# Two transformer layers with a mixture of experts: weights re-laid in DRAM as the chunks of one load, and experts ranked by their rows and packed in double, full, half and quarter tiles

## The chip, the cores and the metric

The kernel runs on one core of a Trainium2 chip. The metric is the device time of one execution in microseconds; its traces are taken by the hardware profiler in an execution of its own. Engines are called as the profile calls them: PE multiplies matrices, PEld loads their stationary operand, DVE, ACT and POOL work on vectors, SP issues most DMAs.

## The reference, cut to what matters

Two layers over 256 latent tokens and 256 context tokens of width 1024. Layer 0 mixes with a gated delta rule beside an S5 scan, layer 1 with latent attention; each layer ends in the same kind of expert stage. Layer 0 sends all 512 tokens through it, layer 1 the 256 latent ones only.

```python
def grouped_moe(h, router_w, router_bias, w_gate, w_up, w_down):
    tok = h.reshape(-1, h.shape[-1])
    scores = jax.nn.sigmoid((tok @ router_w).astype(F32))
    ...                                   # best group of 4 experts, then TOP_K = 2 experts in it
    gates = jnp.sum(jax.nn.one_hot(idx, N_EXPERTS, dtype=F32) * wts[..., None], axis=1)
    out = jnp.zeros(tok.shape, F32)
    for e in range(N_EXPERTS):            # 16 experts, w_gate and w_up 1024 x 512, w_down 512 x 1024
        act = jax.nn.silu(tok @ w_gate[e]) * (tok @ w_up[e])
        out = out + gates[:, e:e + 1] * (act @ w_down[e])
    return out.reshape(h.shape).astype(h.dtype)
```

Everything is fp32. One expert's weights are 6.29 MB, all of a layer's 100.7 MB. With the inputs used, the experts of layer 0 get 36, 55, 46, 43, 99, 80, 71, 52, 72, 47, 27, 58, 132, 51, 78 and 77 rows in the order of their numbers, and those of layer 1 get 23, 44, 31, 6, 47, 60, 50, 17, 34, 11, 42, 45, 17, 19, 27 and 39 (counted from the reference).

## The kernel before, in words

The program is one stream: adaLN vectors, the mixer of layer 0, `moe_route` and `experts0`, the mixer of layer 1, `moe_route` and `experts1`, a final norm. A scheduler puts the instructions of each engine in an order before the launch; within an engine they run in that order. Weights come through rings of buffers of 8 KB per partition (`chunk()`, tag `ch`, 1 MB each): `load_chunk` (L199) takes the next buffer of the ring and issues the load on SP, which stands there until the buffer is free. In layer 0's expert stage nine buffers serve the weights, in layer 1's eighteen.

All loads of big weights fetch from the matrix in its own layout: partition p of a chunk of w_gate takes rows p, 128+p, 256+p and 384+p, 512 columns each, so 2 KB at a time from rows that lie next to each other (`gate_up_chunk`); for w_down the 2 KB are halves of 4 KB rows (`down_chunk`). The input projection (`w_in_load`) takes 512 B at a time, its u part 1 KB. The adaLN weights ada_w alone come as whole rows, 8 KB for each partition.

`moe_route` computes, with many small operations on DVE and a few matmuls, every token's two experts, the row counts `num`, and each row's place in the tiles (`dif`, `val`, `rank`). Then come `tok`, `gate` and row lists for each tile (`m.toki`, `m.gate`, `m.rowi`).

**Layer 0** (`experts0`) has 17 tiles of 128 rows: one per expert, and two for one expert with over 128 rows, which changes places with expert 8 (`BIGP`). A tile's rows are gathered from DRAM (`gather`, on POOL's queue), transposed on PE (`turn`, L203) and split in a rounded part and a remainder (`split`, tags `sp`). Each weight chunk is split too (`wsplit`: `hi` on ACT at L1660, `lo` on DVE or POOL at L1661), in three pairs of buffers (`HI`), and three matmuls replace one (`mm3`). A chunk of 128x2048 is four slices, so it takes 12 matmuls of 512 columns, an expert 72. The rows go back to DRAM with a scatter (`write`); the last tile's are added by matmul (`put_back`). The line `first = wsplit(...)` puts the split of the first chunk ahead of the first tile's own work.

**Layer 1** (`experts1`) has 8 tiles, each of two experts with up to 64 rows. It does not split: PE multiplies fp32 directly from the loaded chunk, one expert on 64 columns of the array, the other on the other 64 (`half`, `p[c, :]` with `j.mw` = 64). The rows are picked with one-hot matmuls (`pick`, `sl,h2k` in the trace), and added back the same way (`put_back`, `y,sT`).

Rows above an expert's capacity (128 or 64) go to overflow tiles in a loop with a count read at run time (`overflow_loop`, up to `NOV` = 7 rounds). With the counts above it runs zero rounds. In layer 0 the ids of 14 places are read from `m.exi` into a register of SP (`expert_id`, a TENSOR_LOAD); all others, and all ids of layer 1, are constants in the program.

Of the kernel before, what the change touches and what calls it, by code (L numbers as in the profile page):

```python
# [31 lines left out]
NOV = 7  # L32
# [4 lines left out]
BIGP = 8  # L37
# [58 lines left out]
def lay(a):  # L96
# [10 lines left out]
    o["w_in"] = f["ab_w_in"][0]  # L107
# [30 lines left out]
    o["q_up"] = f["mla_w_q_up"][0]  # L138
    o["kv_up"] = f["mla_w_kv_up"][0]
    o["mla_wo"] = f["mla_w_out"][0]  # L140
# [3 lines left out]
    o["wg"] = f["moe_w_gate"].reshape(32, 1024, 512)  # L144
    o["wu"] = f["moe_w_up"].reshape(32, 1024, 512)
    o["wd"] = f["moe_w_down"].reshape(32, 512, 1024)
# [14 lines left out]
def _build(es, tc, I, O):  # L161
# [29 lines left out]
    def load_chunk(src, shape, eng=nc.sync):  # L191
        n = 1
        for s in shape[1:]:
            n *= s
        t = chunk()
        v = t[:, :n]
        if len(shape) == 3:
            v = v.rearrange("p (a b) -> p a b", a=shape[1])
        eng.dma_start(v, src)  # L199
        return v  # L200
# [405 lines left out]
    def w_in_load(c0, n, rows=slice(0, D), tile=lambda: cw.tile([128, 1024], F32, tag="raw", bufs=1, name=nm("raw"))):  # L606
        w = tile()
        nc.sync.dma_start(w.rearrange("p (k n) -> p k n", n=n),
                          I["w_in"][rows, c0:c0 + n].rearrange("(k p) n -> p k n", p=128))
        return w  # L610

    def w_in_cols(c0, n, eng):
        return [w.rearrange("p (k n) -> p k n", n=n) for w in split_w(w_in_load(c0, n), eng)]
# [10 lines left out]
    with tc.tile_pool(name="xi1", bufs=1) as xi1, tc.tile_pool(name="ar", bufs=ARB) as arp:  # L624
# [4 lines left out]
        def norm0():  # L629
            for t in range(NT):  # L630
# [12 lines left out]
        uw = [w_in_load(2064 + hh * 256, 256, slice(512 * kh, 512 * kh + 512), tile)  # L643
              for hh, kh, tile in ((0, 0, chunk), (0, 1, chunk), (1, 0, chunk), (1, 1, chunk))]
# [318 lines left out]
    def glu():  # L963
        gluw = [load_chunk(I["glu_w"][:, n * 256:(n + 1) * 256].rearrange("(k p) n -> p k n", p=128), [128, 4, 256])
                for n in range(2)]
# [261 lines left out]
    def out_proj0(opening, after):  # L1227
        with tc.tile_pool(name="op0", bufs=1) as op, tc.tile_pool(name="oq0", bufs=3) as oq:
# [6 lines left out]
            def parts(n, h):  # L1235
                raw = load_chunk(I["w_out"][h * 512:(h + 1) * 512, n * 512:(n + 1) * 512].rearrange(
                    "(k p) n -> p k n", p=128), [128, 4, 512])
# [28 lines left out]
    def out_proj1(opening, after):  # L1266
        with tc.tile_pool(name="op1", bufs=1) as op, tc.tile_pool(name="oq1", bufs=3) as oq:
            def parts(n, h):
                raw = load_chunk(I["mla_wo"][h * 512:(h + 1) * 512, n * 512:(n + 1) * 512].rearrange(
                    "(k p) n -> p k n", p=128), [128, 4, 512])  # L1270
# [27 lines left out]
    def moe_open(l, stack):  # L1298
# [41 lines left out]
        if l == 0:  # L1340
            m.xes = [m.mo.tile([128, D], F32, name=f"xe{i}") for i in range(3)]
            for t in m.xes:
                G.memset(t, 0.0)
            m.io16 = m.mo.tile([128, 16], F32, name="io16")
            m.far = m.mo.tile([128, 16], F32, name="far")
            G.tensor_copy(m.io16, sm[:, SM_IO16:SM_IO16 + 16])
            G.tensor_scalar(m.far[:, 0:BIGP], m.io16[:, 0:BIGP], 16.0 - BIGP, None, op0=OP.add)
            G.tensor_scalar(m.far[:, BIGP:16], m.io16[:, BIGP:16], float(BIGP), None, op0=OP.subtract)
            G.memset(m.far[:, 0:2], -1.0)
        else:  # L1350
            m.h2 = [m.mo.tile([128, D], F32, name=nm("h2k")) for _ in range(2)]
        return m
# [31 lines left out]
    def moe_route(m):  # L1384
        l, n, mo = m.l, m.n, m.mo
        cap = CAP0 if l == 0 else CAP1
        nst = 17 if l == 0 else 8
# [67 lines left out]
        t16, ovn, ovs, dif = rt([128, 16]), rt([128, 16]), rt([128, 16]), rt([128, 16])  # L1455
        if l == 0:


            key, kmx, big, ep = rt([128, 16]), rt([128, 1]), rt([128, 16]), rt([128, 16])
            V.scalar_tensor_tensor(key, num, float(cap), m.far, op0=OP.is_gt, op1=OP.mult)  # L1460
            red(kmx, key, OP.max)
            V.tensor_scalar(big, m.far, kmx, None, op0=OP.is_equal)
            V.tensor_scalar(key[:, 0:1], kmx, 16.0 - BIGP, -16.0, op0=OP.is_ge, op1=OP.mult)
            V.scalar_tensor_tensor(m.io16[:, BIGP:BIGP + 1], kmx, float(BIGP), key[:, 0:1], op0=OP.add, op1=OP.add)
            V.scalar_tensor_tensor(key, m.io16, float(BIGP), big, op0=OP.subtract, op1=OP.mult)
            tt(ep, m.io16, key, OP.subtract)
            m.exi = rt([128, 16], I32, True)
            V.tensor_copy(m.exi, ep)
            first, caps = rt([128, 16]), rt([128, 16])
            V.scalar_tensor_tensor(first, ep, float(BIGP), ep, op0=OP.is_gt, op1=OP.add)  # L1470
            V.tensor_scalar(caps, big, 128.0, 128.0, op0=OP.mult, op1=OP.add)
            V.scalar_tensor_tensor(num, big, -128.0, num, op0=OP.mult, op1=OP.add)
        V.tensor_scalar(ovn, num, float(cap), None, op0=OP.is_gt)
        for j in range(1, 3 if l == 0 else 2):
            V.scalar_tensor_tensor(ovn, num, float(cap + 128 * j), ovn, op0=OP.is_gt, op1=OP.add)
# [23 lines left out]
        V.scalar_tensor_tensor(rin, tid, -128.0, rin, op0=OP.mult, op1=OP.add)  # L1499

# [75 lines left out]
    def gate_up_chunk(l, name, e, hh):  # L1576
        return load_chunk(wsrc(l, name, e)[hh * 512:(hh + 1) * 512, :].rearrange(
            "(k p) n -> p k n", p=128), [128, 4, 512])

    def down_chunk(l, e, nh):  # L1580
        return load_chunk(wsrc(l, "wd", e)[:, nh * 512:(nh + 1) * 512].rearrange(
            "(k p) n -> p k n", p=128), [128, 4, 512])

    def overflow_loop(m, w2, body):

        nreg = nc.values_load(m.novi[0:1, 0:1], min_val=0, max_val=NOV,
                              skip_runtime_bounds_check_because="at most 7 tiles can overflow")
        with tc.For_i(0, nreg, 1) as it:  # L1588
# [3 lines left out]
            body(it + m.nst, e)  # L1592

# [6 lines left out]
    def open_rg2():  # L1600
# [11 lines left out]
    def experts0(m):  # L1612
        with ExitStack() as st:
# [19 lines left out]
            def split(name, p, n):  # L1633
# [10 lines left out]
                return hi, lo  # L1644

# [54 lines left out]
            def half(u, name, hh, parts=None):  # L1700
# [490 lines left out]
```

## Time and profile before

| | before |
|---|---|
| time, median of 3 runs | 1413.93 us (1410.01 to 2414.91) |
| the profiled execution's own time | 1414.94 us |
| its span | 1412.7 us, granted clock 0.942 |
| PE busy | 1251.5 us, 89% |
| DVE, ACT, POOL busy | 56%, 37%, 27% |
| DMA | 340.40 MB, mean 241 GB/s |
| packets | 201805, of them 70638 under 2 KB and 201201 under 8 KB |
| layer 0's expert stage, first row transposes to last tile | 605 to 932 us |
| layer 1's, first expert matmul to last | 1161 to about 1400 us |

The page cuts the span into 40 slices of 35.3 us and gives each engine's busy share in tenths; PEclk is the clock granted to PE, in tenths of full speed. The view by windows gives the same for chosen stretches, in us from the span's start, with the number of instructions in brackets. In the timeline a row is a run of like instructions: start, length, engine, line, operation, output and inputs, tile shape (rows by columns of the array and elements), count, and in square brackets the idle time before it with what ended it. An fp32 matmul on the loaded chunk counts as two there.

### The profile page before, as it was taken

How to read it: one execution, taken by the hardware profiler on the slowest of the kernel's cores; microseconds unless marked ns; L12 is line 12 of the kernel's file. 1: busy time of each engine (PE TensorE's matmuls, PEld its weight loads, DVE VectorE, ACT ScalarE, POOL GpSimd, SP SyncE). 2: the span in 40 equal slices, each digit the busy share in tenths (PEclk: the TensorE clock that was granted, in tenths of full speed). 3: DMA queues.
4: the chain of work that ended last, by engine and by line, in shares of the span. 5: the costliest groups of instructions: out<-in, count | busy, mean ns of one | idle time of the engine just before them, and what ended most of it. 6: DMA issues, size and time to landing. Idle time of an engine off the chain costs nothing. (4 is left out here: it accounts for less than half of the span.)

```text
span 1412.7 us, 18172 instructions
## 1 busy us (share of the span) xinstructions
PE 1251.5 (89%) x6716; PEld 847.8 (60%) x6716; DVE 787.6 (56%) x1460; ACT 529.6 (37%) x775; POOL 381.0 (27%) x266
## 2 busy tenths in 40 slices
PE   5889989899788999589999999976999669999996
PEld 1786655555327988457777777744777544444422
DVE  5776756844974465767775577775566151221112
ACT  3312634544112242167776477724365011000100
POOL 1443434320126330334443233353231020000000
PEclk9999999899798999789999999998999779999998
DMA  8713457767488345679999699753034569999980
GB/s 306 257 34 88 155 171 221 225 216 235 149 251 281 131 172 180 273 244 345 377 369 330 227 317 358 283 210 113 32 135 155 194 254 385 398 401 400 399 336 31
DMA packets 201805, 340.40 MB, mean 241 GB/s; under 512 B 31726, under 2 KB 70638, under 8 KB 201201
## 3 DMA queue, kind: packets, MB, share of 16 engines
q1 hardware_dynamic: 171952, 310.97, 62.3%
q10 hardware_dynamic: 23920, 16.95, 3.9%
q0 software_dynamic: 5840, 11.28, 2.2%
q8 instruction: 55, 0.90, 0.3%
q14 instruction: 38, 0.30, 0.1%
HBM read 320.56 MB, written 27.82 MB: 247 GB/s over the span
## 5 line engine op out<-in xcount | busy, mean ns | idle before, releaser
L206 PE MATMUL ps<-hi,sp 128*128 128x512 f32 x816 | 269.5, 404 | 6.0 <-ACT sp L1640 3.7
L1661 DVE TENSOR_TENSOR lo<-ch,hi 128x2048 fp32r<-128x2048 f32 x80 | 185.1, 2330 | 84.6 <-ACT hi L1660 79.8
L1660 ACT ACTIVATE hi<-ch 128x2048 fp32r<-128x2048 f32 x96 | 184.1, 1920 | 80.3 <-PE ps L206 52.8
L206 PEld LDWEIGHTS ps<-hi,sp 128*128 128x128 f32 x816 | 154.0, 190 | 42.7 <-ACT sp L1640 4.4
L206 PE MATMUL ps<-lo,sp 128*128 128x512 f32 x408 | 164.9, 404 | 3.2 <-DVE lo L1661 2.4
L206 PE MATMUL ps<-ch,stat 128*32 128x512 f32 x384 | 93.9, 646 | 31.7 <-DMA ch<-in_ada_w 30.6
L206 PE MATMUL ps<-ch,xT 128*64 128x512 f32 x480 | 119.7, 596 | 0.0
L1661 POOL TENSOR_TENSOR lo<-ch,hi 128x2048 fp32r<-128x2048 f32 x16 | 73.9, 4621 | 160.6 <-ACT hi L1660 160.6
L206 PEld LDWEIGHTS ps<-lo,sp 128*128 128x128 f32 x408 | 77.8, 191 | 26.9 <-DVE lo L1661 8.8
L206 PEld LDWEIGHTS ps<-ch,xT 128*64 128x64 f32 x480 | 36.1, 137 | 66.5 <-issue 65.2
L228 POOL TENSOR_TENSOR frs<-rs,sm 128x1 f32<-128x1 f32 x2 | 1.1, 560 | 259.8 <-DVE rs L227 259.8
L1867 ACT ACTIVATE aT<-ps 128x512 f32<-128x512 f32 x8 | 4.8, 597 | 149.1 <-PE ps L203 149.1
L206 PE MATMUL ps<-ch,aT 128*64 128x512 f32 x240 | 60.0, 596 | 0.7 <-ACTq L1588 0.7
L1880 DVE TENSOR_TENSOR y<-ps,bcm 128x512 f32<-128x512 f32 x16 | 11.1, 691 | 81.8 <-PE ps L206 81.8
L603 POOL TENSOR_TENSOR wl<-raw,wh 128x1024 fp32r<-128x1024 f32 x16 | 38.7, 2417 | 66.2 <-ACT wh L602 66.0
L206 PE MATMUL ps<-hH,wh 128*128 128x512 f32 x128 | 55.0, 430 | 0.0
L206 PEld LDWEIGHTS ps<-ch,stat 128*32 128x32 f32 x384 | 13.6, 112 | 67.7 <-DMA ch<-in_ada_w 35.0
L206 PE MATMUL ps<-hL,wh 128*128 128x512 f32 x128 | 53.8, 420 | 0.0
L206 PE MATMUL ps<-hH,wl 128*128 128x512 f32 x128 | 53.1, 415 | 0.0
L742 DVE SCALAR_TENSOR_TENSOR ac<-ps,convw,ac 128x510 f32<-128x510 f32 (+1 forms) x48 | 35.5, 740 | 23.7 <-ACT ac L738 23.3
L1152 POOL TENSOR_TENSOR ch<-ch,ch 128x512 fp32r<-128x512 f32 (+1 forms) x28 | 31.1, 1127 | 58.3 <-ACT ch L1151 32.3
L206 PE MATMUL ps<-y,sT 128*128 128x512 f32 x80 | 40.9, 642 | 6.4 <-DVE y L1880 2.3
(543 smaller groups left out, 2559.7 us busy)
## 6 DMA issues: line engine op xcount, KB each, us to landing
ch<-in_wg SPq DMA_DIRECT2D x63, 1024.0 KB
ch<-in_wd SPq DMA_DIRECT2D x62, 1024.0 KB
ch<-in_wu SPq DMA_DIRECT2D x61, 1024.0 KB
ch<-in_ada_w SPq DMA_DIRECT2D x88, 512.0 KB
raw<-in_w_in SPq DMA_DIRECT2D x16, 512.0 KB
bcm<-modd ACTq DMA_DIRECT2D x12, 512.0 KB
x<-in_xs SPq DMA_DIRECT2D x8, 512.0 KB
yd<-x SPq DMA_DIRECT2D x8, 512.0 KB
```

The lines of the kernel that those rows point to most:

```text
L206: return T.matmul(out, l, r, start=start, stop=stop)
L228: G.tensor_tensor(out, t, bc(neghalf, [128, n]), op=OP.pow)
L603: eng.tensor_tensor(wl, w, wh.bitcast(F32), op=OP.subtract)
L742: V.scalar_tensor_tensor(ac[:, :, lo:hi], pv[:, :, lo + o:hi + o], convw[:, blk, j:j + 1], ac[:, :, lo:hi], op0=OP.mult, op1=OP.add)
L1152: eng.tensor_tensor(lo, src, hi.bitcast(F32), op=OP.subtract)
L1660: last_split[:] = (S.activation(hi, w, AF.Copy), eng.tensor_tensor(lo, w, hi.bitcast(F32), op=OP.subtract))
L1661: eng.tensor_tensor(lo, w, hi.bitcast(F32), op=OP.subtract))
L1867: S.activation(j.aT.rearrange("p k n -> p (k n)"), p, AF.Copy)
L1880: V.tensor_tensor(j.y[:, nh], p, g2[:, nh * 512:(nh + 1) * 512], op=OP.mult)
```

## The change

It has two parts.

**Layout.** `cut()` re-lays w_in, its u part (now `w_inu`), glu_w, w_out, mla_w_in, q_up, kv_up, mla_wo and the three expert weights on the host side of the program, before the launch, as blocks of 128 partitions by the contiguous elements of one load. A chunk of expert weights is then one contiguous MB, 8 KB for each partition; the w_in blocks are 4 KB for each partition. ada_w is unchanged. The number of loads, their bytes and the buffers in SBUF stay.

```diff
+    def cut(w, k, n):
+        r, c = w.shape[-2] // (128 * k), w.shape[-1] // n
+        b = w.reshape(-1, r, k, 128, c, n).transpose(0, 1, 4, 3, 2, 5)
+        return np.ascontiguousarray(b).reshape(-1, r, c, 128, k * n)
+    o["w_in"] = cut(w_in[:, 0:2048], 8, 128)[0, 0]
...
-    o["wg"] = f["moe_w_gate"].reshape(32, 1024, 512)
+    for n, w in (("wg", "gate"), ("wu", "up"), ("wd", "down")):
+        o[n] = cut(f["moe_w_" + w].reshape((32,) + f["moe_w_" + w].shape[2:]), 4, 512).reshape(32, 256, 2048)
...
     def gate_up_chunk(l, name, e, hh):
-        return load_chunk(wsrc(l, name, e)[hh * 512:(hh + 1) * 512, :].rearrange(
-            "(k p) n -> p k n", p=128), [128, 4, 512])
+        return load_chunk(wsrc(l, name, e)[hh * 128:(hh + 1) * 128, :], [128, 4, 512])
```

**Packing.** `moe_route` ranks the experts by their row counts (`key`, `cmp`, `pos`), those of `STATIC = (2, 4)` first whatever they hold: experts 0 and 1 in layer 0, 0 to 3 in layer 1. The rank is the place. `caps` and `first` give a place its capacity and first row.

Layer 0 has 13 tiles. Place 2, the fullest, has two tiles for itself (capacity 256), places 3 to 9 one each (128), and places 0 and 1, 10 and 11, 12 and 13, 14 and 15 share a tile, 64 rows each. In a shared tile nothing is split: `whole()` only copies the transposed rows, and `pair()` multiplies in fp32 directly from the loaded chunk, one expert on each 64 columns, as layer 1 does. The order is: places 0 and 1, 10 and 11, the double tile, 12 and 13, places 3, 4, 5, then 14 and 15, then 6, 7, 8, 9. The line `first` is gone.

Layer 1 has 7 tiles: places 0 to 11 in six tiles of two, and places 12 to 15 in one tile of four, 32 rows each, in the order 0, 1, 2, 3, 6, 4, 5 (6 is the tile of four). The experts' ids of all but the static places are now read at run time in layer 1 too.

With the counts above, layer 0's places hold 36 and 55; 132; 99, 80, 78, 77, 72, 71, 58; 52, 51, 47, 46, 43, 27. Layer 1's hold 23, 44, 31, 6; 60, 50, 47, 45, 42, 39, 34, 27; 19, 17, 17, 11. So the overflow loop runs zero rounds again.

```diff
+        V.scalar_tensor_tensor(key, num, 16.0, m.tie, op0=OP.mult, op1=OP.add)
+        tt(cmp, bc(key[:, None, :], SQ), bc(key[:, :, None], SQ), OP.is_gt)
+        red(pos[:, :, None], cmp, OP.add)
...
+        tt(oh, bc(sm[:, SM_IO16:SM_IO16 + 16, None], SQ), bc(pos[:, None, :], SQ), OP.is_equal)
+        tt(oh, oh, bc(sm[:, None, SM_IO16:SM_IO16 + 16], SQ), OP.mult)
+        red(key[:, :, None], oh, OP.add)
+        m.exi = rt([128, 16], I32, True)
+        V.tensor_copy(m.exi, key)
...
+            def whole(name, p, n):
+                o = w2.tile([128, n, 128], F32R, tag=f"{name}h", name=nm("wh")).bitcast(F32)
+                for i in range(n // 4):
+                    S.activation(o[:, 4 * i:4 * i + 4], p(i).rearrange("p (k n) -> p k n", k=4), AF.Copy)
+                return o
...
+            def pair(p, xT, k0, ws, n):
+                for q in range(4):
+                    for b, w in enumerate(ws):
+                        c = slice(64 * b, 64 * b + 64)
+                        mm(p[c], xT[:, k0 + q, c], w[:, q, :], k0 + q == 0, k0 + q == n - 1)
...
-            order = [[t] for t in range(BIGP)] + [[BIGP, BIGP + 1]] + [[t] for t in range(BIGP + 2, m.nst)]
+            one = {p: ([p], [p]) for p in range(3, 10)}
+            order = [([0], [0, 1]), ([10], [10, 11]), ([1, 2], [2]), ([11], [12, 13]), one[3], one[4], one[5],
+                     ([12], [14, 15]), one[6], one[7], one[8], one[9]]
...
-            first = wsplit(gate_up_chunk(0, "wg", 0, 0), V)
             fetch(1)
-            with tc.issue_after(last_split[0].ins), tc.issue_after(last_split[1].ins):
-                unit(0)
-                unit(1)
+            unit(0)
+            unit(1)
...
+            order = [0, 1, 2, 3, 6, 4, 5]
+            def fixed(i):
+                ti = order[i]
                 c = slice(ti, ti + 1)
-                return job([2 * ti, 2 * ti + 1], lambda kk, i: m.ohT[:, kk, i, c], m.tokf[:, c], m.gate[:, c])
+                return job([lambda p=p: who(p) for p in ((2 * ti, 2 * ti + 1) if ti < 6 else range(12, 16))],
+                           lambda kk, i: m.ohT[:, kk, i, c], m.tokf[:, c], m.gate[:, c])
```

Outside the two routes and the two expert stages every engine has the same instructions in the same order, with other sources in the loads. Inside them PE has 3484 rows in all instead of 3898, DVE 1318 instead of 1380, ACT 673 instead of 749, SP 624 instead of 540.

PE at the start of layer 0's experts, before: `xe` are the gathered rows, `hi` and `lo` the split weights, `sp` the split rows.

```order
L203 MATMUL ps_5017<-cm,xe_4487 128x128 x4
L203 MATMUL ps_5024<-cm,xe_4487 128x128 x4
L206 MATMUL ps_5050<-hi_5005,sp_5015 128x512
L206 MATMUL ps_5050<-lo_5006,sp_5015 128x512
L206 MATMUL ps_5087<-hi_5083,sp_5015 128x512
L206 MATMUL ps_5087<-lo_5084,sp_5015 128x512
L203 MATMUL ps_5033<-cm,xe_4488 128x128 x4
```

The same place after: `ch` are chunks as loaded, `wh` the copied rows.

```order
L208 MATMUL ps_5010<-cm,xe_4487 128x128 x4
L208 MATMUL ps_5016<-cm,xe_4487 128x128 x4
L208 MATMUL ps_5023<-cm,xe_4488 128x128 x4
L211 MATMUL ps_5038<-ch_5039,wh_5009 64x512
L211 MATMUL ps_5038<-ch_5041,wh_5009 64x512
L211 MATMUL ps_5038<-ch_5039,wh_5009 64x512
L208 MATMUL ps_5029<-cm,xe_4488 128x128 x4
```

The first matmuls of an expert no longer stand behind a split of a weight chunk on ACT and DVE; half of the second tile's transposes have moved ahead of them.

SP around the first expert loads of layer 0, from the last of four loads of the adaLN weight that stand among them, before:

```order
L199 DMA ch_4983<-in_ada_w 128x2048
L199 DMA ch_5152<-in_wg 128x4x512
L199 DMA ch_5190<-in_wd 128x4x512
L199 DMA ch_5252<-in_wu 128x4x512
L1595 TENSOR_LOAD rt_4823
L199 ISA
L199 DMA ch_5276<-in_wg 128x4x512
```

The same place after:

```order
L204 DMA ch_4983<-in_ada_w 128x2048
L204 DMA ch_5066<-in_wu 128x2048
L204 DMA ch_5076<-in_wu 128x2048
L1607 TENSOR_LOAD rt_4850
L204 ISA
L204 DMA ch_5098<-in_wg 128x2048
L1607 TENSOR_LOAD rt_4850
```

Before, ten loads of layer 0's expert weights stand ahead of the first read of an id; after, the eight of the first tile's gate and up weights. The next ones stand behind ids that the route computes.

PE in layer 1's tile of four, after: the last four of the first half of the gate matmuls, the transposes of the tile ahead of it (`act`), and the start of the second half and of the next tile's picking (`sl,h2k`). Before, each tile has two chunks in turn there, `64x512`.

```order
L211 MATMUL ps_9211<-ch_9215,xT_9120 32x512
L211 MATMUL ps_9211<-ch_9220,xT_9120 32x512
L211 MATMUL ps_9211<-ch_9225,xT_9120 32x512
L211 MATMUL ps_9211<-ch_9230,xT_9120 32x512
L208 MATMUL ps_9249<-cm,act_9208 128x128 x4
L211 MATMUL ps_9211<-ch_9255,xT_9120 32x512
L211 MATMUL ps_9286<-sl_9279,h2k_8421 128x128
```

Four experts now take turns on strips of 32 columns, so the tile has twice as many matmul instructions as a tile of two.

More of the change, by code (lines that the diff above doesn't have):

```diff
@@ L31 @@
 CAP1 = 64
-NOV = 7
+NOV = 8
 RG = 5
@@ L194, in load_chunk @@
             n *= s
[L195 to L200, printed above, removed]
+        v = chunk()[:, :n]
+        three = v.rearrange("p (a b) -> p a b", a=shape[1]) if len(shape) == 3 else v
+        eng.dma_start(v if len(src.shape) == 2 else three, src)
+        return three
     def tp(out, in_, n=128):
@@ L604, in split_w, with w_in_load @@
         return wh, wl
[L606 to L609, printed above, removed]
+    def w_in_load(src, w):
+        nc.sync.dma_start(w, src)
         return w
     def w_in_cols(c0, n, eng):
-        return [w.rearrange("p (k n) -> p k n", n=n) for w in split_w(w_in_load(c0, n), eng)]
+        raw = w_in_load(I["w_in"][c0 // n], cw.tile([128, 1024], F32, tag="raw", bufs=1, name=nm("raw")))
+        return [w.rearrange("p (k n) -> p k n", n=n) for w in split_w(raw, eng)]
     def mm3(p, ah, al, bh, bl, start, stop):
@@ L642, in _build @@
         slots[0], slots[1] = [mring], 0
-        uw = [w_in_load(2064 + hh * 256, 256, slice(512 * kh, 512 * kh + 512), tile)
-              for hh, kh, tile in ((0, 0, chunk), (0, 1, chunk), (1, 0, chunk), (1, 1, chunk))]
+        uw = [w_in_load(I["w_inu"][kh, hh], chunk()) for hh in range(2) for kh in range(2)]
         u_first = split_w(uw.pop(0), G)
@@ L1473, in moe_route @@
-        V.tensor_scalar(ovn, num, float(cap), None, op0=OP.is_gt)
-        for j in range(1, 3 if l == 0 else 2):
-            V.scalar_tensor_tensor(ovn, num, float(cap + 128 * j), ovn, op0=OP.is_gt, op1=OP.add)
+        key, pos, first, caps = (rt([128, 16]) for _ in range(4))
+        cmp, oh = (t[:, i:i + 256].rearrange("p (a b) -> p a b", a=16) for i in (0, 256))
+        SQ = [128, 16, 16]
+        V.scalar_tensor_tensor(key, num, 16.0, m.tie, op0=OP.mult, op1=OP.add)
+        tt(cmp, bc(key[:, None, :], SQ), bc(key[:, :, None], SQ), OP.is_gt)
@@ L1476, in moe_route @@
+        tt(num, num, caps, OP.subtract)
+        V.tensor_scalar(ovn, num, 0.0, None, op0=OP.is_gt)
+        for j in range(1, 4 if l == 0 else 2):
+            V.scalar_tensor_tensor(ovn, num, float(128 * j), ovn, op0=OP.is_gt, op1=OP.add)
         V.tensor_tensor_scan(ovs, ones[:, 0:16], ovn, 0.0, op0=OP.mult, op1=OP.add)
@@ L1592, in overflow_loop, with experts_of, get @@
             body(it + m.nst, e)
+    def experts_of(m):
+        ids = {p: p for p in range(STATIC[m.l])}
+        def get(p):
+            if p not in ids:
+                ids[p] = expert_id(m.exi[0:1, p:p + 1])
+            return ids[p]
+        return get
     def expert_id(ap):
@@ L1760, in experts0 @@
                 for hh in range(2):
-                    half(unit(0), name, hh, first if (name, hh) == ("wg", 0) else None)
-            for i in range(16):
+                    half(unit(0), name, hh)
+            for i in range(len(order)):
                 cur = unit(i)
@@ L1769, in experts0 @@
                             g2[c] = bc_mod(w1, 0, c, 5, f"g2{c}")
[L1770 to L1771 removed]
+                fetch(tiles.index(order[i][0][-1]) + 3)
+                nxt = unit(i + 1) if i + 1 < len(order) else None
                 if nxt:
@@ L1774, in experts0 @@
                 for j in cur:
-                    j.aT = split("a", turn(j.a), 4)
+                    j.aT = (whole if len(j.es) == 2 else split)("a", turn(j.a), 4)
                 if nxt:
                     half(nxt, "wg", 1)
-                    if i < 14 and len(nxt) == 1:
-                        job(order[i + 2][0], i + 2)
+                    if i + 2 < len(order) and len(nxt) == 1:
+                        job(order[i + 2][0][0], order[i + 2][1])
                     write(cur)
```

139 lines of the change are left out of this document (64 added, 75 removed).

## The prediction

> **What bounds the kernel now.** I began with the page's strip of 40 slices, each 35.3 us.
>
> ```profile
> PE   5889989899788999589999999976999669999996
> PEclk9999999899798999789999999998999779999998
> GB/s 306 257 34 88 155 171 221 225 216 235 149 251 281 131 172 180 273 244 345 377 369 330 227 317 358 283 210 113 32 135 155 194 254 385 398 401 400 399 336 31
> ```
>
> PE is busy nearly throughout, so what shortens PE's queue shortens the kernel, if the data keep up. In two stretches PE and the DMAs are full together: slices 18 to 26 (layer 0's experts) and 33 to 38 (layer 1's). The windows put numbers to them (us, busy time with count of PE, PEld, DVE, ACT, POOL, clock, DMA share, GB/s):
>
> ```profile
> 605.70:932.00 326.30, 313.90 (x1396) 245.84 (x1396) 226.18 (x150) 232.15 (x194) 123.80 (x46) 0.98 0.86 307
> 613.80:769.70 155.90, 154.64 (x698) 122.00 (x697) 111.27 (x74) 116.44 (x97) 57.93 (x23) 0.99 0.98 353
> 1200.00:1360.00 160.00, 158.38 (x728) 63.24 (x724) 31.89 (x57) 11.94 (x20) 0.00 (x0) 1.00 1.05 400
> 584.00:598.00 14.00, 1.22 (x10) 0.77 (x9) 13.22 (x70) 0.26 (x1) 4.88 (x3) 0.50 1.02 422
> ```
>
> In layer 0's stage PE is busy 154.6 of 155.9 us, in layer 1's 158.4 of 160.0. The DMA share is about 1 in both, but at three different rates: 353, 400 and, in the last row, 422 GB/s. That last stretch is the route of layer 0, while the first expert chunks in 2 KB pieces and adaLN weights in 8 KB pieces come in.
>
> Next the timeline, for the price of one tile in each stage.
>
> ```profile
> 880.52 0.60 PE L203 MATMUL ps<-cm,xe 128*128 128x128 f32 x4
> 889.41 0.63 PE L206 MATMUL ps<-hi,sp 128*128 128x512 f32 x2
> 890.11 0.63 PE L206 MATMUL ps<-hi,sp 128*128 128x512 f32 x2
> 899.18 0.60 PE L203 MATMUL ps<-cm,xe 128*128 128x128 f32 x4
> 1160.67 0.64 PE L206 MATMUL ps<-x,xT 128*64 128x512 f32 x1
> 1160.67 0.64 PE L206 MATMUL ps<-ch,xT 128*64 128x512 f32 x1
> 1161.15 0.59 PE L206 MATMUL ps<-x,xT 128*64 128x512 f32 x1
> 1181.91 0.66 PE L203 MATMUL ps<-cm,act 128*128 128x128 f32 x4
> 1210.94 0.65 PE L203 MATMUL ps<-cm,act 128*128 128x128 f32 x4
> 1218.88 7.09 PE L206 MATMUL ps<-ch,aT 128*64 128x512 f32 x32
> 1225.80 7.04 PE L206 MATMUL ps<-ch,xT 128*64 128x512 f32 x32
> ```
>
> A full tile of layer 0 takes 899.18 - 880.52 = **18.66 us** from one tile's transposes to the next's. Three matmuls take 890.11 - 889.41 = 0.70 us, 72 of them 16.8, and 1.86 are left for transposes. 17 x 18.66 = 317.2 us, the whole stage. In layer 1 two matmuls on 64 columns start together (1160.67 twice) and the next pair 0.48 us later, 0.43 in steady flow (7.04 / 16). A tile takes 1210.94 - 1181.91 = **29.03 us**.
>
> **The change part by part.** *Layer 0's tiles.* A shared tile costs gate and up at 7.04 each, down at 7.09 and transposes of 1.86: 23.0 us for two experts, where two full tiles cost 37.3. I take layer 1's rows because the instruction is the same: fp32, 64 columns, 512 elements. So 9 x 18.66 + 4 x 23.0 = 259.9 us against 317.2: **-57.3**.
>
> *Start of layer 0.* Before, the first matmuls stand behind splits:
>
> ```profile
> 607.90 0.50 PE L206 MATMUL ps<-hi,sp 128*128 128x512 f32 x1 [1.40 <-ACT sp L1640]
> 610.21 0.79 PE L206 MATMUL ps<-lo,sp 128*128 128x512 f32 x1 [1.81 <-DVE lo L1661]
> 790.43 0.50 PE L206 MATMUL ps<-hi,sp 128*128 128x512 f32 x1 [1.61 <-ACT sp L1640]
> 792.88 0.73 PE L206 MATMUL ps<-hi,sp 128*128 128x512 f32 x2 [1.71 <-DVE sp L1641]
> ```
>
> A shared tile needs one copy on ACT and no weight split, so steady flow begins at about 608 instead of 613: **-5** (0 to -6). At 790 the tile pair of expert 8 has stalls of 1.6 and 1.7 us with a lowered clock between; now a shared tile follows it, which waits for no remainder: **-2** (0 to -5).
>
> *Supply of layer 0.* Eight chunks are in at the start, the ring holds nine. A shared tile eats 12 chunks (12.6 MB) in 23 us, 547 GB/s, more than any window shows; a full tile six in 18.66, 337 GB/s; the double tile six in 37. Two bounds follow. First the ring: at 400 GB/s a chunk comes every 2.62 us, 8.8 in 23 us, so the first two shared tiles take the stock from 8 to 4.8 and to 1.6, and the double tile fills it again; at 353 (7.7 in 23 us) the stock runs out in the second, and each shared tile waits a few us. Second the sum: the stage moves 326.3 x 307 = 100.1 MB now, some 97 with four tiles' rows fewer, and 97 MB in 260 us are 373 GB/s; at 353 they take 275 us. So the term lies between 0 and +22 (15 by the sum, 7 for the ring). Which rate holds? Share 0.98 at 353 scales to 378 at the share of 1.05 that layer 1 reaches, and larger pieces raise that by 422/1.02 over 400/1.05, 8.6%, to 411. Both lie above 373, so I stay near the lower end, at **+5**.
>
> The Trainium skill, "DMA: Bandwidth & Descriptors", "Why small descriptors are slow (HBM only)", gives a fixed overhead of about 3 cycles a packet besides one cycle per 32 B. By it 2 KB pieces cost 67 cycles for 64 and 8 KB pieces 259 for 256, so the new layout would be worth 3.4% and not 8.6%: 391 GB/s here, still above 373, and the +5 would stand. The trace's 422 against 400 is 5.5%, between the two, though its pieces are mixed.
>
> *The route.* DVE works it off in one chain:
>
> ```profile
> 585.10 0.42 DVE L1433 TENSOR_TENSOR cmp<-rt 128x256 f32<-128x256 f32 x1
> 586.05 2.55 DVE L1435 TENSOR_TENSOR cmp<-cmp,sm 128x256 f32<-128x256 f32 x1
> 588.63 0.69 DVE L1401 TENSOR_REDUCE rt<-cmp 128x64 f32<-128x512 f32 x1
> 590.72 0.17 DVE L1460 SCALAR_TENSOR_TENSOR rt<-rt,far 128x16 f32<-128x16 f32 x1
> ```
>
> Small operations follow each other every 0.1 us or so. Layer 0 loses ten small ones and gains ten small ones, three on 256 elements (0.33 to 0.42 each) and two reductions (some 0.35 each): **+1.8**; if one on 256 elements takes 2.55 as the second row did, +4, and 0.5 if part of it fits into gaps of DVE. Layer 1 gains the same five and seven small ones: **+2.5** (1.5 to 5). PE has nothing else to do then (window 584 to 598, 1.2 us busy), so both count in full.
>
> *Ids at run time.* 12 more reads in layer 1, 14 in layer 0 as before:
>
> ```profile
> L1595 SPq TENSOR_LOAD <-rt x14: 265/274/472, 608.8 to 879.4; - x14
> 1164.35 0.37 SPq L199 DMA_DIRECT2D x<-in_wu  x1
> 1351.68 8.85 SPq L199 DMA_DIRECT2D ch<-in_wd  x4
> ```
>
> 0.27 us each on SP, beside loads already queued: 0. Uncovered, each would cost that 0.27 and delay every load behind it; in layer 0 the ninth chunk now waits for the route's ids, some 2.5 us of supply that the +5 holds.
>
> *Layer 1's tiles.* Seven instead of eight: **-29.0**. The tile of four has twice the instructions. The trace has strips of 32 columns in the adaLN matmuls, at the end of layer 0's route:
>
> ```profile
> 600.17 4.85 PE L206 MATMUL ps<-ch,stat 128*32 128x512 f32 x32
> 600.17:605.02 4.85, 4.85 (x36) 1.15 (x34) 0.79 (x6) 1.64 (x1) 4.21 (x4) 0.74 0.57 181
> ```
>
> 32 rows in 4.85 us at clock 0.74 are 3.59 at full clock; four strips at a time in 8 passes of 0.43 would be 3.44. So four run at once and the tile of four costs what a tile of two costs: 0 to **+0.5**. If strips ran only two at a time, it would be +21.
>
> *Supply of layer 1.* 18 of the 96 chunks are in when the ring's second turn begins, at 1164.35. The other 78 take 78 x 1.0486 / 0.400 = 204.5 us and end at 1369, which fits the last issues at 1351.68.
>
> ```profile
> 1388.34 0.66 PE L203 MATMUL ps<-cm,act 128*128 128x128 f32 x4 [0.85 <-DVE act L1860]
> 1396.10 3.65 PE L206 MATMUL ps<-ch,aT 128*64 128x512 f32 x14
> ```
>
> Now PE's last down matmuls follow at 1390 to 1400; 29 us earlier they want their chunks from 1361 on. And the tile of four, fifth in order, eats 24 chunks instead of 12: when it is through, at 1160.7 + 5 x 29 = 1306, 72 are eaten, and at 400 GB/s 18 + 142 / 2.62 = 72 are in. So at 400 PE waits at both places, some 9 us (up to 12). At 422 the loads take 193.8 us, 75 are in at 1306, and the last at 1358: no wait. I take **+0.3** (0 to +12).
>
> *Earlier stages.* w_in, w_out and the attention weights come in larger pieces.
>
> ```profile
> PE ps L206 <- DMA ch<-in_ada_w: 30.6, 18, 14.8
> ACT wh L602 <- DMA raw<-in_w_in: 9.8, 4, 4.2
> DMA packets 201805, 340.40 MB, mean 241 GB/s; under 512 B 31726, under 2 KB 70638, under 8 KB 201201
> ```
>
> PE's DMA waits there are for adaLN weights, which keep their layout; only the 9.8 us of ACT are for w_in, and ACT is seldom what PE waits for. **-2** (0 to -8).
>
> *The sum.* Layer 0: -57.3 - 5 - 2 + 5 + 1.8 = -57.5. Layer 1: -29.0 + 0.5 + 2.5 + 0.3 = -25.7. Earlier -2. Together -85.2. The profiled execution took 1414.94 us (span 1412.7 and 2.2 around it), so 1329.7; it stands 1.0 above the median, so about **1329 us**.
>
> **The rivals.**
>
> *B, the loads gate both stages.* The mechanism: layout brings nothing, 353 GB/s holds in layer 0, 400 in layer 1. Then +22 instead of +5 and +9 instead of +0.3, and the dearer routes (+5): 1360 us. For it speaks that the share is 0.98 at 353 already; against it that PE there used just what it could eat (337 GB/s of weights), so that 353 may be its demand and no limit. The Trainium skill, "DMA: Bandwidth & Descriptors", "Specifications", has a limit of about 358 GB/s from HBM for one core; by it this rival is what happens. The trace's 400 GB/s over 160 us of layer 1 speaks against the page.
>
> *C, more than the sum.* No waits for loads, both splits gone, and w_in's smaller packet count lets layer 0's opening run ahead: -57.3 - 6 - 5 + 0.5, -29 + 1.5, -8: -103, 1311 us.
>
> *D, slower than before.* A chunk whose partitions lie one behind the other may put all 16 DMA engines on neighbouring addresses and stream more slowly than pieces spread over the matrix. The stages need 179 MB (97, and 82 for the 78 chunks) in 552 us (326, and 226 from 1164 to the last down matmuls) to stand where they stood: it decides from 324 GB/s down, and at 300 GB/s the two take 597 us, +45: 1459 us. Against it: the adaLN weights lie in rows of 8 KB and shared a window of 422 GB/s.
>
> *E, the packing does not fit.* An overflow round in layer 0 costs at least 18.7 us and holds its loads behind a register; about 35 with its own start. One round gives 1364, three undo the gain. Against it: the counts fit all places in both layers.
>
> **How the numbers follow.** A 0.62 with its own range of 1312 to 1350, B 0.20, C 0.10, D 0.04, E 0.04. The range from 1308 to 1366 takes in A, C, B and one overflow round. 2% is 28 us, about what a measurement of this kernel can tell from no change; faster by more than that holds in A, B, C and most of E: 0.93; within it 0.03, slower 0.04.
>
> **What would show it.** Steps between row transposes of 18.7 us in nine tiles and 23.0 in four; layer 0's stage from 326 to about 267 us, layer 1's shorter by 26; the tile of four between two `act` transposes at 29 to 30 us; rates above 400 GB/s in both stages. PE waits on `ch<-in_wg`, `in_wu` or `in_wd` of over 15 us would show B; an unchanged step of a shared tile near 37 us, or the tile of four near 50, would make the prediction wrong in its largest terms.

## The result, and the profile after

The changed kernel takes 1368.74 us, median of 4 runs (1365.63 to 1373.91), against 1412.68 us of before beside it: ratio **0.9699**, 95% interval 0.9658 to 0.974. It is faster by 44 us where 85 were forecast, and outside the stated range of 1308 to 1366. The profiled execution took 1368.28 us, its span is 1366.5, the granted clock 0.931 instead of 0.942.

The page's strip of the changed kernel, slices of 34.2 us:

```profile
PE   4889989899777999869998887876999668999996
GB/s 300 262 51 66 155 153 244 222 217 271 137 229 265 228 59 218 205 316 419 414 303 409 327 307 338 292 185 148 31 134 99 268 206 273 424 425 425 424 425 89
```

Layer 1's stage (last slices) runs nearly as forecast, with PE full and 425 GB/s. Layer 0's does not: in slices 21 to 26 (counted from 0, as in the prediction) PE falls to 7 and 8 tenths, while the loads are down at 292 to 338 GB/s in slices 22 to 25. Neither is at its limit there.

Four rows on PE cut the program into parts that both kernels have: the first row transposes of layer 0's experts, layer 1's first transposes (`xn`), the router's first matmuls of layer 1 (`rw,cols`) and the first picking of its experts (`sl,h2k`). Before, and after:

```profile
604.95 0.65 PE L203 MATMUL ps<-cm,xe 128*128 128x128 f32 x4
962.48 3.67 PE L203 MATMUL ps<-cm,xn 128*128 128x128 f32 x16 [7.72 <-DVE rs L227]
1117.88 3.57 PE L206 MATMUL ps<-rw,cols 128*128 128x16 f32 x16 [13.46 <-DMA cols<-modd]
1155.01 5.73 PE L206 MATMUL ps<-sl,h2k 128*128 128x128 f32 x32 [1.79 <-DVE sl L1824]
```

```profile
600.00 0.65 PE L208 MATMUL ps<-cm,xe 128*128 128x128 f32 x4
938.53 3.68 PE L208 MATMUL ps<-cm,xn 128*128 128x128 f32 x16 [7.64 <-DVE rs L232]
1092.23 3.57 PE L211 MATMUL ps<-rw,cols 128*128 128x16 f32 x16 [12.22 <-DMA cols<-modd]
1132.70 6.18 PE L211 MATMUL ps<-sl,h2k 128*128 128x128 f32 x32 [1.82 <-DVE sl L1857]
```

| part | before | after | difference | forecast |
|---|---|---|---|---|
| up to layer 0's experts, with the route | 604.95 | 600.00 | -5.0 | -0.2 |
| layer 0's experts | 357.53 | 338.53 | **-19.0** | **-59.3** |
| layer 1's mixer | 155.40 | 153.70 | -1.7 | 0 |
| layer 1's route | 37.13 | 40.47 | +3.3 | +2.5 |
| layer 1's experts | 257.69 | 233.80 | -23.9 | -28.2 |

The miss lies in layer 0's experts, 40.3 us; the other parts miss by 5 us or less and nearly cancel. The windows of that part, before and after:

```profile
604.95:962.48 357.53, 331.86 (x1449) 255.48 (x1445) 249.50 (x174) 236.27 (x201) 137.43 (x51) 0.97 0.85 302
```

```profile
600.00:938.53 338.53, 287.47 (x1209) 176.60 (x1205) 155.89 (x106) 136.73 (x130) 86.00 (x35) 0.94 0.81 317
```

PE's busy time fell by 44.4 us, but its idle time doubled, from 25.7 to 51.1, and its clock fell from 0.97 to 0.94. The waits of PE in that part, after (us in total, times, longest), say for what:

```profile
PE ps L211 <- POOL lo L1679: 21.6, 8, 4.1
PE ps L211 <- ACT hi L1678: 8.0, 4, 2.6
PE ps L211 <- DVE lo L1679: 3.3, 4, 1.8
```

For the split of weight chunks, 33 us of it; before, waits for `hi` and `lo` came to 3.6. No row says that PE waited for a chunk.

The timeline shows two kinds. Inside a run of full tiles, PE's rows, then ACT's, then POOL's:

```profile
743.79 0.60 PE L208 MATMUL ps<-cm,act 128*128 128x128 f32 x4
747.01 0.60 PE L208 MATMUL ps<-cm,xe 128*128 128x128 f32 x4
756.16 0.51 PE L211 MATMUL ps<-lo,sp 128*128 128x512 f32 x1 [2.30 <-POOL lo L1679]
764.41 0.60 PE L208 MATMUL ps<-cm,act 128*128 128x128 f32 x4
...
747.65 0.60 ACT L1651 ACTIVATE sp<-ps 128x512 fp32r<-128x512 f32 x1 [0.81 <-PE ps L208]
749.52 1.92 ACT L1678 ACTIVATE hi<-ch 128x2048 fp32r<-128x2048 f32 x1
...
751.52 4.58 POOL L1679 TENSOR_TENSOR lo<-ch,hi 128x2048 fp32r<-128x2048 f32 x1 [1.45 <-ACT hi L1678]
```

A full tile takes 20.6 us (743.79 to 764.41) instead of 18.66. In each tile POOL computes one remainder, that of the up weight's first chunk, and needs 4.6 us for it; it ends 2.3 us after PE wants it. It starts late because ACT made the chunk's `hi` at 749.52, behind the copies of the next tile's rows. Before, `hi` stands ahead of those copies, and POOL's remainder is there in time:

```profile
880.71 1.92 ACT L1660 ACTIVATE hi<-ch 128x2048 fp32r<-128x2048 f32 x1 [0.84 <-PE ps L206]
...
882.72 4.62 POOL L1661 TENSOR_TENSOR lo<-ch,hi 128x2048 fp32r<-128x2048 f32 x1 [10.31 <-ACT hi L1660]
```

The second kind is at the border from a shared tile to a full one:

```profile
728.68 0.51 PE L211 MATMUL ps<-hi,sp 128*128 128x512 f32 x1 [2.61 <-ACT hi L1678]
733.28 0.79 PE L211 MATMUL ps<-lo,sp 128*128 128x512 f32 x1 [4.10 <-POOL lo L1679]
...
726.14 0.69 ACT L1764 ACTIVATE y<-ps,rt 128x512 f32<-128x512 f32 x1 [2.70 <-PE ps L211]
726.73 5.50 ACT L1678 ACTIVATE hi<-ch 128x2048 fp32r<-128x2048 f32 x3
```

ACT's queue holds the split of the full tile's up weights behind the copy of the shared tile's last result, and that copy waits for PE. PE runs dry for 2.6 and 4.1 us, and the matmul behind takes 0.79 instead of 0.40 us. The clock of that stretch and of the next tile:

```profile
733.00:740.00 7.00, 6.72 (x19) 5.35 (x20) 4.58 (x2) 1.57 (x1) 0.23 (x1) 0.62 0.99 399
745.00:765.00 20.00, 17.70 (x83) 14.17 (x82) 15.14 (x10) 13.93 (x12) 8.72 (x3) 1.00 0.95 361
```

So the stall of 4.1 us cost some 2.7 us more behind it (an estimate: 7 us at 0.62), a stall of 2.3 us inside a tile nothing more. The Trainium skill, "TensorE: Matmul & The Clock Gate", "Part 1: The HAM clock gate", puts the fall to half rate behind an idle window of about 3.4 us. The trace agrees in part: 0.62 behind 4.1 us and 1.00 around 2.3, but the clock fell as well behind a stall of 3.12 us (0.50 from 674 to 676 us) and behind three of 1.56, 0.30 and 0.69 us close together (0.50 from 648 to 653).

### The profile page after: what moved, and what is told of

Its sections match the earlier page's. It is cut to its first block, busy times and chain, and to the rows that moved or that the text cites. A ratio compares the mean times of both kernels' runs of the same rounds, so it can differ in the third digit from the quotient of the medians.

```text
span 1366.5 us, 17491 instructions
## 1 busy us (share of the span) xinstructions
PE 1178.6 (86%) x6432; PEld 755.0 (55%) x6432; DVE 693.0 (51%) x1398; ACT 424.1 (31%) x699; POOL 326.6 (24%) x250
## 5 line engine op out<-in xcount | busy, mean ns | idle before, releaser
L211 PE MATMUL ps<-hi,sp 128*128 128x512 f32 x432 | 148.4, 419 | 8.8 <-ACT hi L1678 8.0
L1679 DVE TENSOR_TENSOR lo<-ch,hi 128x2048 fp32r<-128x2048 f32 x40 | 108.3, 2735 | 78.9 <-ACT hi L1678 78.9
L211 PE MATMUL ps<-lo,sp 128*128 128x512 f32 x216 | 91.6, 424 | 24.9 <-POOL lo L1679 21.6
L211 PE MATMUL ps<-ch,xT 128*64 128x512 f32 (+1 forms) x488 | 109.3, 596 | 0.0
L211 PEld LDWEIGHTS ps<-hi,sp 128*128 128x128 f32 x432 | 86.1, 201 | 32.5 <-ACT hi L1678 11.7
L1678 ACT ACTIVATE hi<-ch 128x2048 fp32r<-128x2048 f32 x48 | 91.1, 1915 | 27.3 <-issue 23.0
L211 PE MATMUL ps<-ch,wh 128*64 128x512 f32 x384 | 91.8, 597 | 0.0
L211 PEld LDWEIGHTS ps<-lo,sp 128*128 128x128 f32 x216 | 43.6, 202 | 41.5 <-POOL lo L1679 25.0
L211 PE MATMUL ps<-ch,aT 128*64 128x512 f32 (+1 forms) x232 | 52.1, 596 | 0.7 <-ACTq L1590 0.7
L1679 POOL TENSOR_TENSOR lo<-ch,hi 128x2048 fp32r<-128x2048 f32 x8 | 36.5, 4557 | 65.4 <-ACT hi L1678 65.4
```

The lines of the kernel that those rows point to most:

```text
L211: return T.matmul(out, l, r, start=start, stop=stop)
L1678: last_split[:] = (S.activation(hi, w, AF.Copy), eng.tensor_tensor(lo, w, hi.bitcast(F32), op=OP.subtract))
L1679: eng.tensor_tensor(lo, w, hi.bitcast(F32), op=OP.subtract))
```

## Experiments

Theory S: in layer 0 PE waits for splits, because the order that the scheduler gave ACT for the new mix of tiles puts them late. Theory L, rival B of the prediction: the loads are the bound.

**The layout alone**, with the tiling of before (only `lay()` and the loads changed).

> The tiling of before (17 and 8 tiles) with the new layout of the weights. Theory S (in layer 0 PE waits for splits of weight chunks, not for loads; the new packing broke their timing): the layout gives only the 5 us that the stages ahead of layer 0's experts gained in the changed kernel and 1 or 2 later, so 1405 to 1410 us, with both expert stages as long as before. Theory L (loads are what the stages lack): layer 0's stage gets shorter by over 5 us by the layout alone, time under 1400.

1412.93 us, ratio 0.9997 (0.9972 to 1.0022): nothing, and so neither theory's time. Layer 0's part took 357.9 us, as long as before, layer 1's 257.9, the opening 605.1; the 5 us that theory S expected of the opening did not come. Yet the loads did get easier. Layer 1's window from 1200 to 1360 us:

```profile
1200.00:1360.00 160.00, 157.53 (x726) 63.29 (x724) 32.61 (x58) 12.47 (x21) 0.00 (x0) 1.00 1.00 414
```

400 GB/s at share 1.05 became 414 at 1.00, and with PE full nobody needed it.

**The packing alone**, with the old layout and the changed kernel's order of instructions on every engine.

> The new packing with the old layout of all weights (pieces of 2 KB and less); every engine has the same order of instructions as in the changed kernel. Theory S: layer 0's stage stays near the changed kernel's 338.5 us (first row transposes to layer 1's first transposes), within 5; the opening is 5 us longer, and layer 1, which then gets 400 instead of 425 GB/s for seven tiles, 5 to 12 longer: 1378 to 1388 us. Theory L: layer 0's stage gets 10 us longer or more, as its loads fall to 353 to 400 GB/s: over 1390 us.

1380.88 us (1374.37 to 1387.13), ratio 0.976 (0.9705 to 0.9815, so whether it is faster by 2% stays open), inside theory S's range. Layer 0's part took 344.3 us, 5.8 more than in the changed kernel, layer 1's 237.4, 3.6 more. PE's wait for POOL in layer 0 is the same to the tenth, and a wait for chunks is new:

```profile
PE ps L206 <- POOL lo L1682: 21.6, 8, 4.1
PE ps L206 <- DMA ch<-in_wu: 4.0, 2, 3.5
```

A stretch inside layer 1's experts shows the layout itself, with PE full in both. Packing alone, then the changed kernel:

```profile
1160.00:1250.00 90.00, 90.00 (x460) 39.54 (x458) 16.51 (x35) 8.97 (x15) 0.00 (x0) 1.00 1.05 398
1160.00:1247.00 87.00, 87.00 (x438) 36.27 (x436) 18.56 (x36) 7.17 (x12) 0.00 (x0) 1.00 1.01 425
```

The two stretches do not start at the same matmul; over the same 438 rows as in the changed kernel (1175.3 to 1262.3 us) the packing alone has 399 GB/s. So the splits' waits do not depend on the loads, and theory L falls for the bulk. The layout is worth some 10 us (9.4 in these two parts, 12 by the medians), but only under the new packing. The opening was 609 us here, more than expected; it differs by up to 9 us between profiles (last section).

**POOL's remainders on DVE**: `V` for `G if (name, hh) == ("wu", 0) else V` in `half`.

> The changed kernel, but the remainder of an up weight's first chunk is computed on DVE (2.3 us) instead of POOL (4.6 us). Theory S: PE's 21.6 us of waits for POOL's remainders fall by 10 to 20 us, some of them turn into shorter waits for DVE or ACT, and the clock granted after them rises: 1346 to 1360 us. Theory L: no change, 1366 to 1371 us, as the chunk itself comes late.

1350.77 us, ratio 0.9562 (0.9514 to 0.9611), 18.0 less than the changed kernel and inside theory S's range. Layer 0's part fell by 22.6 to 315.9 us. POOL's row is gone, and full tiles run at 18.3 us:

```profile
834.87 0.60 PE L208 MATMUL ps<-cm,act 128*128 128x128 f32 x4
853.14 0.60 PE L208 MATMUL ps<-cm,act 128*128 128x128 f32 x4
...
PE ps L211 <- ACT hi L1678: 8.0, 4, 2.6
```

The waits at the borders are left: those for ACT as in the changed kernel, and those for DVE's remainders rose from 3.3 to 7.9 us. DVE as a whole paid nothing for the eight remainders that it took over: its 48 take 109.0 us (2.29 each), the 40 of the changed kernel took 108.3 (2.74 in the mean). There, one that started beside a remainder on POOL was slower; this one ended 2.15 us behind POOL's, as if it had waited for it:

```profile
669.15 4.92 DVE L1679 TENSOR_TENSOR lo<-ch,hi 128x2048 fp32r<-128x2048 f32 x1 [18.98 <-ACT hi L1678]
667.40 4.52 POOL L1679 TENSOR_TENSOR lo<-ch,hi 128x2048 fp32r<-128x2048 f32 x1 [18.61 <-ACT hi L1678]
```

**Splits written ahead at the borders**, POOL kept.

```diff
+                    if len(cur[0].es) == 1 and len(nxt[0].es) == 2:
+                        wd = [wsplit(down_chunk(0, cur[0].es[0](), nh), V) for nh in range(2)]
                     half(nxt, "wg", 0)
...
+                    if len(cur[0].es) == 2 and len(nxt[0].es) == 1:
+                        wu = wsplit(gate_up_chunk(0, "wu", nxt[0].es[0](), 0), V)
-                    write(cur)
-                    half(nxt, "wu", 0)
+                    write(cur, wd)
+                    half(nxt, "wu", 0, wu)
```

> The changed kernel, but where a full tile meets a shared one the splits are written ahead: the down chunks of a full tile ahead of the next shared tile's gate matmuls, and the first up chunk of a full tile ahead of the shared tile's down matmuls (its remainder on DVE). Theory S: the waits at those five borders (for splits, 2 to 4 us each, some 20 us in all, and the lowered clock behind them) go for the most part: 1345 to 1360 us; the waits inside the runs of full tiles (2.3 us each) stay. Theory L: no change, 1366 to 1371, as the chunk is not there any earlier.

1360.84 us (1356.94 to 1377.48), ratio 0.9622 (0.9556 to 0.9689); layer 0's part 329.1 us, 9.4 less. Waits for POOL went from 21.6 to 10.6 us, but at two borders the wait moved on to the next chunk's split, behind the same copies. That is about half of the 20 us that were expected of the borders.

**Both**, with the second up chunk written ahead too.

> The changed kernel with both: all remainders on DVE, and splits written ahead at the borders between full and shared tiles (both up chunks of a full tile ahead of the shared tile's down matmuls, both down chunks of a full tile ahead of the shared tile's gate matmuls). Theory S: the gains of the two single edits were 22.6 and 9.4 us in layer 0's stage; they share the borders, so 28 to 32 us together: layer 0's stage 306 to 311 us, time 1338 to 1346. If loads take over as the bound (theory L, in its weaker form), waits for chunks appear and the stage stays above 313.

A miss: 1356.78 us, ratio 0.9605 (0.9543 to 0.9667), layer 0's part 321.0 us, 5 more than with DVE alone. Two borders still have the wait, one chunk later, and the new order of PE mixes shared and full matmuls: the window from the double tile's `act` transposes to the next is full in both, and 4.8 us longer here. This run, then the one with DVE alone:

```profile
686.70:718.30 31.60, 31.60 (x139) 17.37 (x139) 7.69 (x7) 11.03 (x12) 3.00 (x3) 1.00 0.79 319
683.50:710.30 26.80, 26.80 (x127) 16.26 (x126) 10.02 (x8) 11.05 (x12) 3.25 (x3) 1.00 0.91 359
```

Writing a split ahead moves more than the split. The two windows don't hold quite the same matmuls, so how much of the 5 us is the mixing stays open.

**Only the order on ACT**: POOL kept, and inside runs of full tiles the next tile's row copies are put behind the split of the up weight's first chunk (the down chunks' splits are written ahead with it).

```diff
+                        wd = [wsplit(down_chunk(0, cur[0].es[0](), nh), V) for nh in range(2)]
+                        wu = wsplit(gate_up_chunk(0, "wu", nxt[0].es[0](), 0), G)
+                        after = tc.issue_after(last_split[0].ins)
...
+                        with after:
+                            job(order[i + 2][0][0], order[i + 2][1])
```

> The changed kernel with POOL's remainders kept; only inside runs of full tiles ACT splits an up weight's first chunk ahead of its copies of the next tile's rows, instead of behind them. Theory S (the place on ACT's queue makes POOL's 4.6 us late by 2.3): the waits for POOL of 2.3 us in the five tiles inside runs go to under 0.7 each, 8 to 12 us in all: 1356 to 1361 us. Rival (POOL itself is too slow for the new stage, wherever it starts): no change, 1365 to 1370.

The time settles nothing: 1367.03 us (1359.66 to 1374.91) lies in the rival's range and misses theory S's. The part does more: 331.8 us, 6.7 less (8 to 12 were expected), while this profile's opening was 6 us longer. PE's order in a full tile is the same as in the changed kernel. The waits for POOL inside the runs fell from 2.3 us to 0.9 in the first and about 0.5 in the second, where full tiles take 18.8 us with POOL still at work:

```profile
852.62 0.60 PE L208 MATMUL ps<-cm,act 128*128 128x128 f32 x4
871.46 0.60 PE L208 MATMUL ps<-cm,act 128*128 128x128 f32 x4
```

So POOL's 4.6 us fit into a full tile when ACT makes the split early enough; the change had moved the place on ACT's queue, POOL was as fast as before. A faster remainder takes the wait away too, as the run with DVE showed.

**Shared tiles in a row**: the four shared ones, the double one, the seven full ones; POOL kept.

> The changed kernel with another order of layer 0's tiles: the four shared ones first, then the double tile, then the seven full ones; POOL's remainders kept. The scheduler then gives ACT the same pattern in the run of full tiles as before the change (split of the up weight's first chunk ahead of the row copies). Theory S: full tiles take 18.7 us again, and two of the five borders are left: 20 to 30 us less for splits; four shared tiles in a row eat 50 MB in 92 us, at 411 to 425 GB/s PE waits 5 to 15 us for chunks: net 1345 to 1360 us. Theory L: the waits for chunks take over 20 us, 1366 or more.

1347.17 us, ratio 0.9546 (0.949 to 0.9602); layer 0's part 316.5 us. Behind the double tile the scheduler falls into the pattern of before. This is ACT's queue in a run of full tiles, in the changed kernel and here (`hi` splits, `sp` or `wh` row copies, `act` the gate, `y` a result):

```
changed kernel: hi hi hi sp hi sp sp act hi y hi y
shared in a row: hi hi hi hi sp hi sp sp act y hi y
```

Its tiles take 18.67 us again. And the row of shared tiles shows what the loads can give:

```profile
793.76 0.60 PE L208 MATMUL ps<-cm,act 128*128 128x128 f32 x4
812.43 0.60 PE L208 MATMUL ps<-cm,act 128*128 128x128 f32 x4
...
640.00:710.00 70.00, 54.99 (x237) 18.68 (x234) 4.77 (x8) 10.33 (x16) 5.05 (x5) 1.00 1.01 421
PE ps L211 <- DMA ch<-in_wu: 6.7, 5, 1.8
PE ps L211 <- DMA ch<-in_wd: 5.2, 4, 1.6
```

421 GB/s, and PE idle for 15 of 70 us. That is the supply term of the prediction made visible, at a rate near the 411 that it had worked out.

**Layer 1's tile of four last**: `order = [0, 1, 2, 3, 4, 5, 6]` in `experts1`.

> The changed kernel with layer 1's tile of four as the last one instead of the fifth. In the changed kernel the two intervals around it took 32.3 and 33.8 us instead of 29.0 without a wait for loads. If the picking of later tiles, which PE does among its matmuls, breaks the four strips' concurrency, six tiles take 29.0 each and the last one runs unbroken: layer 1 gets 4 to 8 us shorter, 1360 to 1364 us. Rival: the 24 chunks are then wanted at the end, where the loads at 425 GB/s have no spare: PE waits there, no gain or up to 10 us lost.

1365.59 us (1362.44 to 1367.41), which overlaps the changed kernel's runs; but layer 1's part is 229.5 us, 4.3 less, and this part took 233.7 to 233.9 in every other run with the changed kernel's layer 1 and layout. In the changed kernel the tile of four had stretched the two intervals after it:

```profile
1243.57 3.64 PE L211 MATMUL ps<-ch,xT 128*32 128x512 f32 x32
1247.14 0.66 PE L208 MATMUL ps<-cm,act 128*128 128x128 f32 x4
1247.73 1.04 PE L211 MATMUL ps<-ch,xT 128*32 128x512 f32 x2
1248.70 0.49 PE L211 MATMUL ps<-sl,h2k 128*128 128x128 f32 x2
1279.41 0.66 PE L208 MATMUL ps<-cm,act 128*128 128x128 f32 x4
```

32.3 us, and 33.8 to the next (1313.17), where 29.0 is a tile of two. One matmul of one strip (two in the count) that stands between full ones takes 1.0 us by itself; side by side, 16 of four experts (32 in the count) take 3.64. Last in order, with less left to pick, 4.3 of these 8 us go; no wait for chunks came instead.

This run also shows how far a single profile can be trusted. Its layer 0, the same instructions as in the changed kernel, took 334.8 us, 3.8 less. All of it lies in the double tile, 40.0 us between `act` transposes instead of 43.9: behind nearly the same short stalls PE's clock stayed at 1.00 there (648 to 654 us), where it had fallen to 0.50 in the changed kernel's profile. So gains of layer 0's part are good to some 4 us; of the 22.6 with the remainders on DVE, where the clock stayed up too, the medians confirm 18.0.

**Combined**: remainders on DVE, order two shared, double, two shared, seven full, tile of four last.

> The changed kernel with three edits: all remainders on DVE, layer 0's tiles in the order two shared, double, two shared, seven full (four borders instead of six, the double tile refilling the ring between the shared ones), and layer 1's tile of four last. Theory S: from the run with all remainders on DVE (layer 0's stage 315.9 us, 1350.8) two borders go, 4 to 5 us of waits each and 2 to 4 behind them for the lowered clock; hardly any wait for chunks comes in place of them (under 4 us): layer 0's stage 300 to 306 us; layer 1 4.3 less as in its own run: 1333 to 1342 us, faster than all runs so far. Theory L: the shared tiles in twos wait for chunks as those in a row of four did (14 us), 1346 or more.

**1330.63 us**, median of 5 (1328.19 to 1337.7), ratio 0.9406 (0.9367 to 0.9444): faster than both kernels and all other runs, and 2 us below the range expected. Layer 0's part 306.1 us, layer 1's 229.5. What is left of layer 0's part and of its waits for splits:

```profile
607.68:913.75 306.07, 279.17 (x1208) 172.58 (x1204) 156.41 (x114) 137.30 (x130) 45.03 (x27) 0.95 0.88 351
PE ps L211 <- ACT hi L1678: 4.5, 3, 2.6
PE ps L211 <- DVE lo L1679: 3.5, 4, 1.5
```

PE is idle for 26.9 us, about as much as before the change (25.7), and its busy time is 52.7 us less than before. That it comes near the forecast of 1329 is no support for the forecast: it needed three edits that the forecast had not thought necessary.

## Why the prediction was right and wrong

**Layer 0's tiles, the step that failed.** The sum priced nine full tiles at 18.66 us and four shared ones at 23.0, as if a tile kept its price next to another kind. The shared ones kept it (620.96 to 644.14 between the first two `act` transposes, 23.2 us). The work went nearly as priced too, 52.7 us in the last run against 57.3. But 18.66 was the price of a tile for which POOL's remainder came with no slack at all; in the changed kernel a full tile took 20.6. In the changed kernel PE wanted POOL's remainder 6.85 us after the row transposes (747.01 to 756.16 - 2.30). Before, that is 880.52 + 6.85 = 887.4, and POOL ended at 882.72 + 4.62 = 887.3. That stood in the trace of before and I did not read it; nor did I compare ACT's order, only PE's and SP's. Of the 40 us missed in this part, 22.6 came back with the remainders on DVE alone, 22.0 with another order of tiles alone, 32.5 with all edits, each good to some 4 us.

**The borders.** The prediction had -5 at the start and -2 at the double tile's exit for splits that go, and nothing for the other four of the five borders between shared and other tiles. (The last expectation counts them as six and four; they are five, and three in that run.) The -5 came: shared matmuls flow from 602 us on, two after the first transposes. So did the -2: from 688.5 to 715.3 us, behind the double tile, PE is full. (The prediction put a lowered clock between the two stalls at 790 of before; it stood behind them, 0.50 from 794 to 796.) But PE waited 6.7 and 6.4 us where a full tile follows a shared one, 4.3 where a shared one follows a full one, 2.5 at the start of the double tile and 3.1 inside it, with a lowered clock behind some of them. "A shared tile waits for no remainder" was right and beside the point, since the splits of the full tiles on either side of it come late.

**Supply of layer 0.** I took +5 with bounds of 0 and +22; PE waited for no chunk. The rate I had worked out, 411 GB/s, was near: 421 in the row of four shared tiles. The 0 end was right for this order of tiles: with the remainders on DVE and the same order PE still waited for no chunk, and in the combined run, with four shared tiles near the start, for one, 1.6 us. Only four of them in a row made the term real.

**Rival B** gave 1360 and the time came out at 1369, but by another mechanism: no limit of 353 or 400 GB/s held. The row had 0.98 at 353 because it was PE's demand, as the text against it said: with the layout alone the stage moved 353 GB/s again, now at a share of 0.93 (620 to 770 us). The Trainium skill's limit of about 358 GB/s from HBM for one core ("DMA: Bandwidth & Descriptors", "Specifications", half of a stack's 716) does not hold here, in a program on one core: 425 GB/s over 87 us. The Trainium skill's fixed cost per packet (same page, "Why small descriptors are slow (HBM only)") gave an estimate of 3.4% for the larger pieces (3.5% as a rate), where the same instructions in layer 1 ran at 399 GB/s with the old layout and 425 with the new, 6.5%.

**Layer 1.** -28.2 forecast, -23.9 measured. The supply was right: 423 to 426 GB/s from 1160 to 1313 us, no wait for chunks. The tile of four was priced at +0.5 and cost 4.3 by its place, as its strips' concurrency is broken by picks in between. The route was +3.3 for +2.5. In layer 0, from the router's last matmuls to the adaLN matmuls, it went from 18.2 to 19.4 us, +1.2 for +1.8.

**Earlier stages** were put at -2 and the opening is 5 us shorter, but the layout alone had it at 605.1 as before; the difference is within what the opening differs between profiles.

**Range and chances.** The upper end was built on loads and an overflow round, the lower on no waits at all. No rival had the splits on ACT and POOL as the new bound of layer 0; that was the missing case. That the kernel gets faster by over 2% came true.

## What to carry to other kernels

A stage in which PE is full can still be one late split away from not being full: before a tile's price is carried over to a new mix, look at how early its inputs are ready, not only at how busy PE is. Compare the order on the helping engines too: what stands ahead of what on ACT decided here, and two orders of the same tiles differ by 22 us in one stage. And a faster load helps only beside something that waits for it: the layout was worth nothing alone and some 10 us under the new packing.

## What the runs showed of the hardware

A stall of 4.1 us on PE was followed by a clock of 0.62 for some 7 us, stalls of 2.3 us by none. Near 3 us it went both ways: behind 3.12 us in the changed kernel the clock fell (0.50 from 674 to 676), behind 3.13 us in the run with the tile of four last it stayed at 1.00 (673 to 681). Matmuls on strips of 32 columns run side by side only while they stand next to each other: one alone takes 1.0 us, 16 of four experts 3.64. A split's remainder takes 2.29 us on DVE; one that started 1.75 us behind a remainder on POOL took 4.92 and ended 2.15 us behind it. The opening up to layer 0's experts took 599.5 to 609.2 us in eleven profiles, among them 599.5 to 607.7 in kernels that differ only behind it; what makes the difference was not followed up.
